# SiLUs of gate behind the last copy out of a bank, and V weights at multiples of 256 bytes, in a neighbourhood-attention and SwiGLU layer

## The chip, the cores and the metric

One core of a Trainium2 chip runs the whole program. The metric is the device time of one execution in microseconds (us). Three runs of the kernel before took 1791.04, 1791.50 and 1793.87 us, so its median is 1791.5.

## The reference

One encoder layer is applied to two groups of tokens with the same parameters, 1024 tokens (`x_prompt`) and 512 (`x_sample`), with 1024 features, 16 heads of 64 and 2816 columns in the feed-forward part. All is float32.

```python
def swiglu(x, w_gate, w_up, w_down):
    return (jax.nn.silu(x @ w_gate) * (x @ w_up)) @ w_down

def run(x):
    h = rms_norm(x, norm_mix)
    x = x + neighbourhood_attention(h, na_w_qkv, na_rpb, na_w_o)
    x = x + swiglu(rms_norm(x, norm_ffn), w_gate, w_up, w_down)
    return rms_norm(x, norm_final)
```

`neighbourhood_attention` projects `h` to q, k and v, and lets each token of a grid 64 wide attend to a window of at most 8 rows and 16 columns, with a bias that depends on the offset. With the depth of one layer that is set here, the other mixers of the reference don't run.

## The kernel before

Tokens are taken in tiles of 128. A float32 matrix is split in two parts, `hi` (rounded, made by a cast on ACT) and `lo` (the rest, a subtraction on DVE; `split`, L155 to L161), and a product is three matmuls for each block of 128 rows: hi hi, hi lo, lo hi (`PASS`, L180). The stages follow one another on TensorE (PE):

- **V projection** (L303 to L341, 10 to 159 us). The norm of twelve token tiles is made and transposed, and `v_tile` (L292) multiplies each by the 512 columns of one half of the V weights, first half `n = 0`, then half `n = 1`: 24 matmuls a tile, with the transposed tokens (`hTp`, `hTs`) as the stationary and the weights (`wv`) as the moving operand of 512 columns. The pool `vpool` (L261) holds in this order `fill` (480 numbers in each partition, the value of a masked bias, written out by DMA at L320), the norm's gains `gb`, two `x`, five `wv0`, five `wv1` and two `vs`. Its first byte is a multiple of 256 in each partition. Raw weights of half `n = 1` come through a pool of two buffers (`rpool`, L164).
- **Attention** (159 to 800 us): q and k projections (L351), scores (L413), transposes (L439), weighted sums (L450), and the output projection (L609).
- **Gate and up** (L934 to L949, 800 to 1460 us). Tokens are in two chunks of 768, the feature blocks in 11 pairs, so there are 22 calls of `unit`, here counted 0 to 21 in the order in which they run. A unit computes a 2 x 2 block product by seven products in place of eight (Strassen's method in Winograd's form), once for gate and once for up (`blocks`, L847). A product is 12 matmuls with a moving operand of 384 columns, and sums are kept in the PSUM banks `pa`, `pb` and `pd`:

| step of `blocks` | PE | out of the bank |
|---|---|---|
| 1 | product 0 into `pa` | ACT copies `pa` to `c11` (L858) |
| 2 | product 1 into `pb` | DVE adds `pb` to `c11` (L861) |
| 3 | product 5 onto `pa` | ACT copies `pa` to `c12` (L865) |
| 4 | product 4 into `pd` | ACT copies `pd` to `c22` (L869) |
| 5 | product 6 onto `pa` | DVE adds `pa` to `c22` (L872) |
| 6 | product 2 onto `pd` | DVE adds `pd` to `c12` (L875) |
| 7 | product 3 onto `pa` | stays there, read by the last SiLU |

 A product that goes on in a bank must wait until what stands there has been read: product 6 for the copy to `c12`, product 2 for the copy to `c22`, product 3 for the add to `c22`. After gate's seventh step `unit` writes the four SiLUs (L892) in the order c11, c12, `pa`, c22 of its list `gs`; after up's it multiplies (L896). GpSimd (POOL) then adds four operands of the next stage (L900 to L903) and issues seven stores (L905). Between the steps `ticks` runs a little of other work: in chunk 0 norms and transposes of chunk 1, in chunk 1 `down_sums` (L770), sums of down's weights on DVE (L784, L786) and POOL (L789, L791). The operands of a block's products are made in `w_ops` (L803): `wa` from one piece of the weights, `ws` from two sums `wt`.
- **Down** (L1063 to L1122, 1460 to 1789 us), 1386 matmuls, again seven products a block.

The order in which each engine takes its instructions is set before the run, by a scheduler that knows what depends on what and may move an instruction ahead of others on the same engine; a dependency of the kind `NoSync` between two instructions of one engine (as in `in_order`, L98, and `pinned`, L110) is no wait of its own, but keeps their order. On the chip an engine takes them one by one, and one that waits holds up those behind it.

Of the kernel before, what the change touches and what calls it, by code (L numbers as in the profile page):

```python
# [11 lines left out]
F32 = mybir.dt.float32  # L12
F32R = mybir.dt.float32r
AF = mybir.ActivationFunctionType
# [4 lines left out]
P = 128  # L19
# [36 lines left out]
def body(tc, xp, xs, g_mix, g_ffn, g_fin, w_qkv, rpb, w_o, w_g, w_u, w_d, yp, ys):  # L56
    nc = tc.nc
# [8 lines left out]
    with es:  # L66
# [43 lines left out]
        def pinned(work, *engines):  # L110

            traced = nc.cur_bb.bb.instructions
            mark = traced[-1]
            done = next(work, 0) == 0
            start = next(k for k in reversed(range(len(traced))) if traced[k] is mark) + 1
            for e in engines:
                own = [i for i in traced[start:] if i.engine == e.engine]
                if own:
                    last = next((i for i in reversed(traced[:start]) if i.engine == e.engine), None)
                    for a, b in zip([last] + own, own):  # L120
                        if a is not None:
                            tc.add_manual_dep(b, a.name, mybir.DependencyInfo(
                                mybir.DependencyClass.NoSync, mybir.DependencyReason.DATA), reason="pinned")
            return done

        def psum(tag, name):
            return ps.tile([P, 512], F32, tag=tag, name=name, bufs=4 if tag == "S" else 2)
# [131 lines left out]


        with tc.tile_pool(name="vpool", bufs=2) as vp:  # L261
            fill = vp.tile([P, 480], F32, tag="fill", name="fill", bufs=1)
            nc.gpsimd.memset(fill, FILL)
            gb = vp.tile([P, D], F32, tag="gb", name="gb", bufs=1)

# [363 lines left out]
        for hp in range(HP):  # L629
# [5 lines left out]
            n = len(jobs[hp])  # L635
# [201 lines left out]
        def product(bank, a, b, start, stop):  # L837
            for k in range(KB // 2):
                for i, (y, z) in enumerate(PASS):
                    nc.tensor.matmul(bank[:, :HT], a(y, k), b[:, z, k], start=start and k == 0 and i == 0,  # L840
                                     stop=k == KB // 2 - 1 and i == 2,
                                     skip_group_check=not start)

        def ctile():
            return fl.tile([P, HT], F32, tag="c", name="c", bufs=13)

        def blocks(w, p, hops, out):  # L847

            ops = w_ops(w, p)
            pa, pb, pd = psum("G", "pa"), psum("V", "pb"), psum("S", "pd")  # L850
            va, vb, vd = pa[:, :HT], pb[:, :HT], pd[:, :HT]

            def go(i, bank, start, stop):
                product(bank, ops[i], hops[i], start, stop)

            go(0, pa, True, False)
            c11 = ctile()
            nc.scalar.copy(c11, va)  # L858
            yield
            go(1, pb, True, True)  # L860
            nc.vector.tensor_tensor(c11, c11, vb, ALU.add)  # L861
            yield
            go(5, pa, False, False)
            c12 = ctile()
            nc.scalar.copy(c12, va)  # L865
            yield
            go(4, pd, True, False)
            c22 = ctile()
            nc.scalar.copy(c22, vd)  # L869
            yield  # L870
            go(6, pa, False, False)
            nc.vector.tensor_tensor(c22, c22, va, ALU.add)  # L872
            yield
            go(2, pd, False, True)
            nc.vector.tensor_tensor(c12, c12, vd, ALU.add)  # L875
            yield
            go(3, pa, False, True)
            out.extend((c11, c12, va, c22))
            yield

        def unit(c, p, hops, tick):
            gs, us = [], []
# [3 lines left out]
            for x in order:  # L886
                next((g, u)[x])
                done[x] += 1
                if not x and done[0] == 7:
                    for n in (0, 1, 3, 2):  # L890
                        o = ctile() if n == 2 else gs[n]
                        nc.scalar.activation(o, gs[n], AF.Silu)  # L892
                        gs[n] = o
                tick()
            for n in (0, 1, 3, 2):
# [156 lines left out]
        c11, c12, c22 = {}, {}, {}  # L1052
# [10 lines left out]
        for q in range(84):  # L1063
            m, tt, h = q // 12, q % 12 // 2, q % 2
            n = SEQ[m]
# [76 lines left out]
```

## Time and profile before

| | |
|---|---|
| median of three runs | 1791.5 us |
| the profiled execution, its own time | 1791.51 us |
| its span, first to last instruction | 1789.4 us |
| mean granted TensorE clock | 0.994 |
| gate and up, first to last matmul | 799.65 to 1460.24 us |
| busy share of ACT / DVE / POOL | 49% / 68% / 25% |

```profile
DVE  4401787778887666677777877877888866546553
ACT  4411667677776455445454434543434335433433
PEclk9999999999999999999999999999999999999999
```

These are three rows of the page's slices: each digit is the busy share of one 40th of the span (44.7 us) in tenths, and the last row is TensorE's granted clock. Neither DVE nor ACT is full in gate and up (digits 18 to 33), so what counts there is whether one of their instructions is late, not how many there are.

In the rows of the timeline that follow below, the columns are start and length in us, the engine, the line of the kernel, the operation, and out<-in by the names of the program; brackets at a row's end give the idle time before it and what ended it.

### The profile page before, as it was taken

The page shows a single profiled execution, that of the slowest core. Times are in us where ns is not written, and L with a number is a line of the kernel's source. Part 1 is how long each engine was busy: PE and PEld are TensorE (multiplying, and loading weights), DVE is VectorE, ACT ScalarE, POOL GpSimd, SP SyncE. Part 2 cuts the span into 40 slices and gives each one's busy share as a digit, 9 for nine tenths or more (in the row PEclk, how much of TensorE's full clock was granted, in tenths as well). Part 3 has the DMA queues.
Part 4 walks back from the last instruction along what each step waited for, and adds up shares of the span by engine and source line. Part 5 has one row for each costly group of instructions (what it writes and reads, how often), then busy time and mean ns, then how long its engine had stood idle before and what let it go on. Part 6 is the DMA issues. An engine that isn't in the chain of part 4 may idle for free.

```text
span 1789.4 us, 25908 instructions
## 1 busy us (share of the span) xinstructions
PE 1735.7 (97%) x9178; PEld 1522.1 (85%) x9178; DVE 1211.5 (68%) x2267; ACT 870.4 (49%) x1742; POOL 439.5 (25%) x509
## 2 busy tenths in 40 slices
PE   7999999999999999999999999999999989999998
PEld 6878777777776878879999999999999978888886
DVE  4401787778887666677777877877888866546553
ACT  4411667677776455445454434543434335433433
POOL 1111000000121000112443424344545462005300
PEclk9999999999999999999999999999999999999999
DMA  7755333333464444554545633554666469555643
GB/s 243 220 173 175 110 104 106 105 113 106 127 195 154 146 133 136 181 161 150 159 151 164 217 112 124 182 171 158 206 228 217 171 218 340 184 166 166 211 119 110
DMA packets 229858, 295.60 MB, mean 165 GB/s; under 512 B 27648, under 2 KB 173824, under 8 KB 229728
## 3 DMA queue, kind: packets, MB, share of 16 engines
q1 hardware_dynamic: 205744, 215.94, 39.3%
q0 software_dynamic: 21248, 69.62, 10.6%
q10 hardware_dynamic: 2736, 8.39, 1.4%
q8 instruction: 72, 1.18, 0.3%
q14 instruction: 58, 0.48, 0.1%
HBM read 218.45 MB, written 87.97 MB: 171 GB/s over the span
## 4 chain that ended last, share of the span: by engine, by line
PE 72%; DVE 10%; DMA 8%; ACT 4%; issue 3%; SPq 1%; POOL 1%; DVEq 0%; ACTq 0%; POOLq 0%
PE pd L1078 17%; PE pa L840 16%; PE pg L351 8%; PE pd L840 8%; PE pgv L297 6%; PE pgo L609 5%; PE pb L840 4%; DMA vr<-v_d 4%; PE pss L413 3%; PE po L450 2%; PE ptt L439 2%; DMA wr<-na_w_qkv 1%; SPq L397 1%; ACT s L424 1%; DVE pT L443 1%
## 5 line engine op out<-in xcount | busy, mean ns | idle before, releaser
L1078 PE MATMUL pd<-wd,go 128*128 128x512 f32 x1386 | 317.9, 392 | 3.8 <-DVE wd L158 3.1
L1078 PEld LDWEIGHTS pd<-wd,go 128*128 128x128 f32 x1386 | 261.9, 189 | 59.8 <-DVE wd L158 4.3
L840 PE MATMUL pa<-h,ws 128*128 128x384 f32 x1056 | 200.0, 337 | 8.0 <-ACT c L865 7.2
L351 PE MATMUL pg<-hTp,whl 128*128 128x512 f32 x768 | 200.7, 405 | 0.0
L840 PE MATMUL pd<-h,ws 128*128 128x384 f32 x1056 | 197.4, 334 | 0.0
L840 PEld LDWEIGHTS pa<-h,ws 128*128 128x128 f32 x1056 | 183.1, 188 | 12.8 <-ACT c L865 10.8
L840 PEld LDWEIGHTS pd<-h,ws 128*128 128x128 f32 x1056 | 184.3, 188 | 0.0
L158 DVE TENSOR_TENSOR ws<-wt,ws 128x1024 fp32r<-128x1024 f32 x88 | 118.5, 1348 | 83.8 <-ACT ws L157 83.7
L351 PEld LDWEIGHTS pg<-hTp,whl 128*128 128x128 f32 x768 | 138.9, 190 | 33.7 <-issue 7.7
L840 PE MATMUL pa<-h,wa 128*128 128x384 f32 x792 | 146.0, 335 | 1.8 <-DVE c L872 1.8
L609 PE MATMUL pgo<-wo,oh 128*128 128x512 f32 x576 | 139.1, 392 | 1.3 <-DVE oh L158 1.3
L840 PEld LDWEIGHTS pa<-h,wa 128*128 128x128 f32 x792 | 137.6, 188 | 2.8 <-DVE c L872 2.7
L424 ACT ACTIVATE s<-s,mx 128x384 f32<-128x384 f32 (+1 forms) x192 | 109.0, 570 | 55.3 <-DVE mx L421 55.3
L157 ACT CAST go<-gr 128x768 fp32r<-128x768 f32 x84 | 65.6, 783 | 137.5 <-PE pd L1078 97.9
L158 DVE TENSOR_TENSOR go<-gr,go 128x768 fp32r<-128x768 f32 x84 | 81.6, 972 | 70.1 <-ACT go L157 68.7
L609 PEld LDWEIGHTS pgo<-wo,oh 128*128 128x128 f32 x576 | 107.4, 188 | 24.6 <-DVE oh L158 1.7
L905 POOL DMA_DIRECT2D gop_d<-c x66 | 50.6, 767 | 304.1 <-DVE c L896 296.9
L158 DVE TENSOR_TENSOR wa<-wr,wa 128x512 fp32r<-128x512 f32 x132 | 112.5, 864 | 18.9 <-ACT wa L157 18.0
L157 ACT CAST ws<-wt 128x1024 fp32r<-128x1024 f32 x88 | 92.5, 1053 | 64.6 <-issue 52.4
L157 ACT CAST wa<-wr 128x512 fp32r<-128x512 f32 x132 | 81.9, 621 | 71.5 <-PE pb L840 43.6
L351 PE MATMUL pg<-hTs,whl 128*128 128x512 f32 x384 | 107.3, 416 | 2.1 <-DVE q L362 2.1
L840 PE MATMUL pb<-h,wa 128*128 128x384 f32 x528 | 98.6, 334 | 0.0
(158 smaller groups left out, 2953.3 us busy)
## 6 DMA issues: line engine op xcount, KB each, us to landing
wr<-ffn_w_gate SPq DMA_DIRECT2D x44, 512.0 KB
wr<-ffn_w_up SPq DMA_DIRECT2D x44, 512.0 KB
wr<-na_w_qkv SPq DMA_DIRECT2D x38, 512.0 KB
gop_d<-gs POOLq DMA_DIRECT2D x88, 192.0 KB, 4.7
gr<-gop_d SPq DMA_DIRECT2D x42, 384.0 KB
gr<-gop_d SPq DMA_DIRECT2D x42, 320.0 KB
gop_d<-c POOLq DMA_DIRECT2D x66, 192.0 KB, 2.7
vr<-v_d SPq DMA_DIRECT2D x192, 64.0 KB
```

Of the source, the lines that this page charges most:

```text
L157: nc.scalar.copy(hi, raw)
L158: nc.vector.tensor_tensor(lo, raw, f32(hi), ALU.subtract)
L297: nc.tensor.matmul(pg, hh[a][:, k, c:c + P], wv[k // 2][b][:, k % 2], start=(k == 0 and i == 0), stop=(k == KB - 1 and i == 2))
L351: nc.tensor.matmul(pg, w[:, a, k, :], h[b][:, k, c:c + 512], start=(k == 0 and i == 0), stop=(k == KB - 1 and i == 2))
L413: nc.tensor.matmul(pt[:, :n], q[h * HD:(h + 1) * HD, a, j].rearrange("p r i -> p (r i)"), kv[:, krow:krow + nrow, BS[j]:BS[j] + 32], start ...
L424: nc.scalar.activation(s[:, :n], s[:, :n], AF.Exp, bias=mx, scale=-1.0, accum_out=sm)
L439: nc.tensor.transpose(pt[:, c * P:(c + 1) * P], s[:, c * P:(c + 1) * P], ident)
L450: nc.tensor.matmul(pos[h][:, g * 256:(g + 1) * 256], vs[c][:, j, h * P:(h + 1) * P], pT[h][:, c].rearrange("p z q -> p (z q)"), start=(c = ...
L609: nc.tensor.matmul(pg, ohs[k // 4][:, a, k % 4], wo[:, b, k, n * 512:(n + 1) * 512], start=(k == 0 and i == 0), stop=(k == KB - 1 and i == 2))
L840: nc.tensor.matmul(bank[:, :HT], a(y, k), b[:, z, k], start=start and k == 0 and i == 0, stop=k == KB // 2 - 1 and i == 2, skip_group_chec ...
L905: nc.gpsimd.dma_start(out=gop_d[i, 3 * c:3 * c + 3, :, p].rearrange("j q t -> q j t"), in_=a.rearrange("q (j t) -> q j t", j=3))
L1078: nc.tensor.matmul(pd, go[:, y, i - a], wds[m, i][:, z], start=(i == 0 and k == 0), stop=(i == NP - 1 and k == 2))
```

## The change

Two edits. In `unit`, each of the four SiLUs of gate is given an order on ACT behind `copied[0]`, which is the last instruction that `blocks` wrote at its fourth step, the copy of `pd` to `c22`; at that place gate's blocks have run and up's have not, so it is gate's own copy. And `fill` is given 512 numbers a partition, of which 480 are used as before, so that every later tile of `vpool` lies 128 bytes further on.

```diff
+        def after(ins, *others):
+
+            for o in others:
+                tc.add_manual_dep(ins.ins, o.ins.name, mybir.DependencyInfo(
+                    mybir.DependencyClass.NoSync, mybir.DependencyReason.DATA), reason="after")
...
-            fill = vp.tile([P, 480], F32, tag="fill", name="fill", bufs=1)
+            fill = vp.tile([P, 512], F32, tag="fill", name="fill", bufs=1)[:, :480]
...
+        copied = [None]
+
...
             c22 = ctile()
-            nc.scalar.copy(c22, vd)
+            copied[0] = nc.scalar.copy(c22, vd)
...
-                        nc.scalar.activation(o, gs[n], AF.Silu)
+                        after(nc.scalar.activation(o, gs[n], AF.Silu), copied[0])
```

In the built programs the `wv` tiles start at byte 115,072 of a partition before and 115,200 after, each next one 4,096 further on: 128 past a multiple of 256 before, on one after. The tiles `hTp`, `whl`, `wo`, `oh`, `wd` and the operands `h`, which the other projections read, start on multiples of 256 in both. PE's, POOL's and SP's instructions stand in the same order as before; ACT's differ in the 22 gates, DVE's in a few of them.

On ACT, a gate without other work beside it (such as that of unit 20), before, from its copy of `pa` to `c11` on. `wa` and `ws` are the cast operands, `c<-pa` and `c<-pd` the copies, ACTIVATE the SiLUs:

```order
L858 COPY c<-pa 128x384
L157 CAST wa<-wr 128x512 x2
L892 ACTIVATE c<-c 128x384
L865 COPY c<-pa 128x384
L869 COPY c<-pd 128x384
L157 CAST ws<-wt 128x1024
L892 ACTIVATE c<-c 128x384
L157 CAST ws<-wt 128x1024
```

The same gate with the change (line numbers are up to 8 higher there):

```order
L866 COPY c<-pa 128x384
L163 CAST wa<-wr 128x512 x2
L873 COPY c<-pa 128x384
L877 COPY c<-pd 128x384
L900 ACTIVATE c<-c 128x384
L163 CAST ws<-wt 128x1024
L900 ACTIVATE c<-c 128x384
L163 CAST ws<-wt 128x1024
```

The first SiLU has moved past both copies; it now stands between the copy to `c22` and the first cast of `ws`. This is so in all gates but those of units 1, 3 and 5.

On ACT, the gate of unit 3, which has two squares of a norm beside it (L696, with the tile numbers 9914 and 9915), before, from behind the first copy:

```order
L892 ACTIVATE c<-c 128x384
L157 CAST wa<-wr 128x512
L865 COPY c<-pa 128x384
L157 CAST wa<-wr 128x512
L869 COPY c<-pd 128x384
L696 ACTIVATE t_9914,ms<-t_9916 128x1024
L696 ACTIVATE t_9915,ms<-t_9917 128x1024
L157 CAST ws<-wt 128x1024
L892 ACTIVATE c<-c 128x384
L157 CAST ws<-wt 128x1024
```

With the change:

```order
L163 CAST wa<-wr 128x512 x2
L873 COPY c<-pa 128x384
L877 COPY c<-pd 128x384
L702 ACTIVATE t_9914,ms<-t_9916 128x1024
L702 ACTIVATE t_9915,ms<-t_9917 128x1024
L900 ACTIVATE c<-c 128x384 x2
L163 CAST ws<-wt 128x1024 x2
```

Here two SiLUs stand behind the squares and ahead of both casts of `ws`.

On DVE, the same gate of unit 3, before, from the add of `pb` on (L861; `me` belongs to the norm):

```order
L861 TENSOR_TENSOR c<-c,pb 128x384
L158 TENSOR_TENSOR wa<-wr,wa 128x512 x2
L698 TENSOR_SCALAR me<-ms 128x1
L872 TENSOR_TENSOR c<-c,pa 128x384
L158 TENSOR_TENSOR ws<-wt,ws 128x1024
L875 TENSOR_TENSOR c<-c,pd 128x384
L698 TENSOR_SCALAR me<-ms 128x1
L158 TENSOR_TENSOR ws<-wt,ws 128x1024
```

With the change:

```order
L869 TENSOR_TENSOR c<-c,pb 128x384
L164 TENSOR_TENSOR wa<-wr,wa 128x512 x2
L704 TENSOR_SCALAR me<-ms 128x1
L880 TENSOR_TENSOR c<-c,pa 128x384
L883 TENSOR_TENSOR c<-c,pd 128x384
L704 TENSOR_SCALAR me<-ms 128x1
L164 TENSOR_TENSOR ws<-wt,ws 128x1024 x2
```

Both adds out of PSUM now stand ahead of both subtractions for `ws`.

## The prediction

> **What bounds the kernel now.** I read the page first, for the engine that is full and for the chain of work that ended last.
>
> ```profile
> PE 1735.7 (97%) x9178; PEld 1522.1 (85%) x9178; DVE 1211.5 (68%) x2267; ACT 870.4 (49%) x1742; POOL 439.5 (25%) x509
> ...
> PE pd L1078 17%; PE pa L840 16%; PE pg L351 8%; PE pd L840 8%; PE pgv L297 6%; PE pgo L609 5%; PE pb L840 4%; DMA vr<-v_d 4%; PE pss L413 3%; PE po L450 2%; PE ptt L439 2%; DMA wr<-na_w_qkv 1%; SPq L397 1%; ACT s L424 1%; DVE pT L443 1%
> ```
>
> PE is the bound, and both edits touch lines that stand high in the chain: V projection (L297) and gate and up (L840). There a shorter matmul, or a stop of PE that goes, counts in full unless something else is late right behind it. Second, the groups, for what stops PE in gate and up:
>
> ```profile
> L840 PE MATMUL pa<-h,ws 128*128 128x384 f32 x1056 | 200.0, 337 | 8.0 <-ACT c L865 7.2 <-ACT c L858 0.8
> ...
> L840 PE MATMUL pa<-h,wa 128*128 128x384 f32 x792 | 146.0, 335 | 1.8 <-DVE c L872 1.8
> ```
>
> The 7.2 us are product 6 waiting for the copy to c12 (L865), the 1.8 us product 3 waiting for the add to c22 (L872). Third, the timeline of one such stop, the gate of unit 21:
>
> ```profile
> 1435.82 2.25 PE L840 MATMUL pd<-h,ws 128*128 128x384 f32 x12
> ...
> 1437.98 0.54 DVE L861 TENSOR_TENSOR c<-c,pb 128x384 f32<-128x384 f32 x1
> ...
> 1438.55 0.52 ACT L892 ACTIVATE c<-c 128x384 f32<-128x384 f32 x1 [4.00 <-DVE c L861]
> 1438.98 0.46 ACT L865 COPY c<-pa 128x384 f32<-128x384 f32 x1
> ...
> 1439.50 2.36 PE L840 MATMUL pa<-h,ws 128*128 128x384 f32 x12 [1.43 <-ACT c L865]
> 1439.71 1.06 ACT L157 CAST ws<-wt 128x1024 fp32r<-128x1024 f32 x1
> 1440.68 1.31 POOL L791 TENSOR_TENSOR t<-t 128x512 f32<-128x512 f32 x1
> 1440.81 2.27 DVE L158 TENSOR_TENSOR ws<-wt,ws 128x1024 fp32r<-128x1024 f32 x1 [1.69 <-ACT ws L157]
> ...
> 1443.00 0.54 DVE L872 TENSOR_TENSOR c<-c,pa 128x384 f32<-128x384 f32 x1
> ...
> 1443.78 2.24 PE L840 MATMUL pa<-h,wa 128*128 128x384 f32 x12
> ```
>
> What the copy reads, product 5, was ready when product 4 began at 1435.82. But ACT stood for 4.00 us at the SiLU, which waits for DVE's late add (L861), and the copy stood behind it. A product takes 2.08 us where nothing stops PE (the chain's row at 813.40 in part 2: 24 matmuls in 4.16), so product 6 was **due** at 1435.82 + 2.08 = 1437.90 and came 1.60 late: the bracket's 1.43 and 0.17 to start again. It also runs 0.12 longer after the stop (2.36, and 2.24 for product 3 at 1443.78).
>
> **Part 1: the SiLU behind the copy to c22.** Nothing is added or removed; the SiLU moves past both copies and now stands ahead of the cast of `ws`, so the new question is what that cast delays: DVE's subtraction for `ws`, and behind it on DVE the add L872, for which product 3 waits. A plain gate without a stop, unit 8, gives the steps:
>
> ```profile
> 1049.55 0.52 ACT L892 ACTIVATE c<-c 128x384 f32<-128x384 f32 x1 [2.39 <-DVE c L861]
> ...
> 1049.98 0.46 ACT L865 COPY c<-pa 128x384 f32<-128x384 f32 x1
> ...
> 1050.51 2.35 PE L840 MATMUL pa<-h,ws 128*128 128x384 f32 x12
> 1050.75 0.48 ACT L869 COPY c<-pd 128x384 f32<-128x384 f32 x1 [0.30 <-issue]
> 1051.13 1.05 ACT L157 CAST ws<-wt 128x1024 fp32r<-128x1024 f32 x1
> 1052.21 1.23 DVE L158 TENSOR_TENSOR ws<-wt,ws 128x1024 fp32r<-128x1024 f32 x1 [2.09 <-ACT ws L157]
> ...
> 1053.35 0.55 DVE L872 TENSOR_TENSOR c<-c,pa 128x384 f32<-128x384 f32 x1
> ```
>
> Call T the start of product 6. Copy to c22 at T + 0.24, next instruction 0.38 later, SiLU 0.43 (start to start), so the cast at T + 1.05 in place of T + 0.62; the subtraction 1.08 later, L872 1.14 after that, T + 3.27; product 3 may start 0.60 after L872 does (unit 18 below), T + 3.87. Due is T + 4.16, so 0.29 us of slack is left and PE hides the move. What such a gate gains is the 0.11 by which its product 6 runs long (2.35): seven gates (8, 9, 10, 12, 13, 14, 19), **0.7 us**. The rest of the stopped gates:
>
> ```profile
> 899.24 2.37 PE L840 MATMUL pa<-h,ws 128*128 128x384 f32 x12 [0.84 <-ACT c L865]
> ...
> 960.61 2.35 PE L840 MATMUL pa<-h,ws 128*128 128x384 f32 x12 [1.05 <-ACT c L865]
> ...
> 1021.25 2.38 PE L840 MATMUL pa<-h,ws 128*128 128x384 f32 x12 [0.33 <-ACT c L865]
> ...
> 1024.27 0.54 DVE L872 TENSOR_TENSOR c<-c,pa 128x384 f32<-128x384 f32 x1
> ...
> 1143.83 0.54 DVE L872 TENSOR_TENSOR c<-c,pa 128x384 f32<-128x384 f32 x1
> ...
> 1257.69 2.36 PE L840 MATMUL pa<-h,ws 128*128 128x384 f32 x12 [0.33 <-ACT c L865]
> ...
> 1258.88 1.30 POOL L789 TENSOR_TENSOR t<-t,t 128x512 f32<-128x512 f32 x1
> 1259.00 2.27 DVE L158 TENSOR_TENSOR ws<-wt,ws 128x1024 fp32r<-128x1024 f32 x1 [1.08 <-ACT ws L157]
> ...
> 1261.19 0.54 DVE L872 TENSOR_TENSOR c<-c,pa 128x384 f32<-128x384 f32 x1
> ...
> 1288.53 2.36 PE L840 MATMUL pa<-h,ws 128*128 128x384 f32 x12 [1.44 <-ACT c L865]
> ...
> 1353.23 0.54 DVE L872 TENSOR_TENSOR c<-c,pa 128x384 f32<-128x384 f32 x1
> ...
> 1353.83 2.37 PE L840 MATMUL pa<-h,wa 128*128 128x384 f32 x12 [1.32 <-DVE c L872]
> ```
>
> - Unit 21. T = 1437.90; SiLU at 1438.55 as before (its add), cast at 1438.98, subtraction at 1440.06, ahead of POOL's add at 1440.68, so it takes the 1.23 of unit 8 and not 2.27. L872 at 1441.20, PE free to go at 1441.80, due 1442.06: no stop, and product 3 comes 1443.78 - 1442.06 = **1.72** earlier. Unit 16 reads alike: **1.72**.
> - Units 3 and 5: 0.84 + 0.17 + 0.12 and 1.05 + 0.17 + 0.12, **2.5**. On DVE L872 now stands ahead of the subtraction for `ws`, which is needed only by up's third product.
> - Unit 7: T = 1020.75, due 1024.91; L872 stays at 1024.27 (no idle time before it, so DVE's own queue sets it) and lets PE go at 1024.87: **0.6**.
> - Unit 15, and 20 like it: T = 1257.20, cast at 1258.25, subtraction at 1259.33 instead of 1259.00. POOL's add holds it up in both (2.27 for 1.23) and ends at 1260.18, so L872 stays at 1261.19; PE goes at 1261.79, not 1261.97: **0.2** each, though 0.49 of stop and more seem to go.
> - Units 11 and 18: L872 at 1143.83 and 1353.23 comes out of a DVE that has no idle time before it, and product 3 waits for it already; a stop only moves from product 6 to product 3: **0**. Unit 17 likewise (and may lose 0.1). Units 0, 1, 2, 4, 6 don't wait here.
>
> Sum: 0.7 + 3.44 + 2.5 + 0.6 + 0.4 = **7.6 us**. Bounds: 10.5 if L872 is never late (nine brackets, 7.2, nine times 0.17 and 0.12, and the plain gates' 0.7), and 4.6 if units 16 and 21 too meet POOL's add and keep 0.2 each. I stay at 7.6, since the subtraction there starts 0.6 before POOL.
>
> The Trainium skill's page "SBUF — State Buffer" (SBUF: two separate sides) says that DVE and GpSimd share a port as an exclusive lock, and the loser waits for the whole instruction. The 2.27 against 1.23 agree; by a port that is shared out instead, units 15 and 20 would gain nothing and the sum would be 7.2.
>
> **Part 2: V's weights on multiples of 256 bytes.** Same instructions; only addresses move. The chain in order of time:
>
> ```profile
> 77.84 4.23 DMA wr<-na_w_qkv
> 84.44 7.75 DMA wr<-na_w_qkv
> 94.64 64.46 PE pgv L297 x275
> 159.10 21.80 PE pg L351 x96
> ...
> 778.03 21.78 PE pgo L609 x96
> ...
> 813.40 4.16 PE pa L840 x24
> ```
>
> With a moving operand of 512 columns PE takes 21.80 / 96 = 227 ns a matmul in q and k projection, 21.78 / 96 = 227 in the output projection, but 64.46 / 275 = 234 in V projection, the only one of the three whose moving tiles start off the 256 bytes. The chain stays on PE through those 64 us. So 7.4 ns x 275 = **2.0 us** in the second half. In the first half the chain runs from PE through two loads of weights (77.84, 84.44) into the second half: what PE gains before about 75 us moves them forward, what it gains later it waits out at 94. From 38 to 75 six tiles of 24 gain some 0.14 each (not every matmul, as each tile is broken by transposes): **0.8 us**. Earlier PE waits for norms. Sum 2.8; bounds 0, if the addresses aren't the cause, and 576 x 7.4 ns = 4.3. Attention starts on loads and biases issued in this stage, which move with it; the loads into the moved tiles I take at nothing (no row has one at both addresses).
>
> **Sum.** The profiled execution took 1791.51 us (span 1789.4), the median is 1791.5, so no correction: 1791.5 - 7.6 - 2.8 = **1781.1**.
>
> **The rivals.**
> - *A, addresses change nothing*: the 7 ns belong to something else in V projection, such as its stationary operand. For it: no row varies the address alone. Against: the stationary tiles (`hTp`) start on 256 in both programs, and all the moving tiles that run at 227 ns do. 1791.5 - 7.6 = 1783.9. The Trainium skill, "SBUF — State Buffer" (Specifications), gives SBUF lines of 16 bytes and a penalty for crossing into a new one; 128 bytes is a whole number of these, so by that rule a run of 2,048 bytes costs the same at both addresses, which is this rival. Its section on operand start alignment says that its runs timed nothing; the 227 against 234 here speak the other way.
> - *B, the stop is handed on*: in units 16 and 21 the subtraction for `ws` starts 0.6 us later than I replay, behind POOL's add; gain there 0.2 each, 4.6 in all, 1791.5 - 4.6 - 2.8 = 1784.1. For it: the cast has only 0.6 us in hand, less than one SiLU and a copy. Against: its inputs are there, and POOL's add comes behind five stores of its own queue.
> - *C, slower*: the SiLU ahead of the cast pushes DVE's subtraction into a POOL instruction in nearly every gate. Then L872 comes at T + 3.27 + 1.04, product 3 is 0.75 late, 22 x 0.75 = 16.5 us, against stops that now cost 7.2 + 1.8 and a dozen restarts of at most 0.29, some 12.5 in all: 4 us lost. With V's 2.8 about 1792.7, without it 1795.5. It decides from about 20 gates on. Against: POOL's adds lie there in units 15 to 18, 20 and 21 only.
> - *D, nothing*: PE's stops were L861's lateness and remain, since other casts hold the copies, and A holds too: 1791.5. Against: in unit 21 ACT sat idle for the 4.00 us ahead of the SiLU, so no cast ahead of it was late.
>
> **How the numbers follow.** Forecast 0.60 (1779 to 1783), A 0.13, B 0.17, C 0.04, D 0.06. 0.2% is 3.6 us, about what a measurement of this kernel can tell from no change. Faster 0.60 + 0.13 + 0.17 = 0.90, same 0.06, slower 0.04. The three runs lie 2.8 us apart, and one stretch at a lower granted clock costs 1.5:
>
> ```profile
> 331.86 4.52 PE pg L351 x12
> 343.17 2.99 PE pg L351 x12
> ```
>
> So the range takes the upper bounds of both parts (1791.5 - 10.5 - 4.3 = 1776.7) at the low end, and A and B and one or two such stretches at the high end: 1776.7 to 1786.5.
>
> **What would show it.** Second half of V projection 62.4 us long and 227 ns a matmul; waits of PE for L865 near 0; waits for L872 up from 1.8 to about 4.3 (units 11, 15, 17, 18, 20); `ws` cast about 0.4 later behind product 6; units 3, 5, 7, 16, 21 near 29.1 us. Wrong, if L872 waits reach 9, if V stays at 234 ns, or if the gain is lost at the start of down (L1078), where loads set the pace.

## The result, and the profile after

The changed kernel took 1783.47 us (median of four runs, 1780.15 to 1785.13) beside 1792.03 for the kernel before (four runs, 1791.04 to 1793.87): a ratio of 0.9948, 95% interval 0.993 to 0.9966, that is 8.6 us less. The ratio is estimated over the runs of both kernels, so it need not be the quotient of two medians. One run of the kernel before, in the rows of e10 and e11 below, took 6000.42 us and is left out of the median there. The changed kernel's profiled execution took 1784.12 us, with a span of 1782.1 (before 1789.4).

Lines have moved by 6 to 8: gate and up's matmul is L846 (before L840), V projection's L303 (L297), the copy to c11 L866 (L858), the add to c11 L869 (L861), the copies to c12 and c22 L873 and L877 (L865, L869), the add to c22 L880 (L872), the SiLU L900 (L892), cast and subtraction of `split` L163 and L164 (L157, L158). From the page of the changed kernel, engines, the chain by line and the two groups of gate and up in which PE waits (busy time, mean ns of one, idle time ahead of it and what ended it):

```profile
PE 1729.5 (97%) x9178; PEld 1521.2 (85%) x9178; DVE 1207.1 (68%) x2267; ACT 870.7 (49%) x1742; POOL 439.1 (25%) x509
...
PE pa L846 18%; PE pd L1086 17%; PE pd L846 8%; PE pg L357 7%; PE pgv L303 6%; DMA vr<-v_d 5%; PE pb L846 4%; PE pgo L615 4%; PE pss L419 3%; DMA wr<-na_w_qkv 2%; SPq L403 2%; PE po L456 2%; PE ptt L445 1%; ACT s L430 1%; DVE pT L449 1%
...
L846 PE MATMUL pa<-h,ws 128*128 128x384 f32 x1056 | 198.0, 335 | 2.3 <-ACT c L866 2.3
...
L846 PE MATMUL pa<-h,wa 128*128 128x384 f32 x792 | 147.2, 337 | 3.6 <-DVE c L880 3.6
```

PE is still the bound and the same lines carry the chain. The 7.2 us for the copy to c12 are gone from the first group; what stands there now, 2.3 for the copy to c11, is another wait (unit 11, below). The wait for the add to c22 has doubled, 1.8 to 3.6. The gate of unit 21, in time:

```profile
1432.92 2.24 PE L846 MATMUL pa<-h,ws 128*128 128x384 f32 x12
1433.00 0.54 DVE L869 TENSOR_TENSOR c<-c,pb 128x384 f32<-128x384 f32 x1
1433.16 0.48 ACT L877 COPY c<-pd 128x384 f32<-128x384 f32 x1 [1.65 <-PE pd L846]
...
1433.58 0.53 ACT L900 ACTIVATE c<-c 128x384 f32<-128x384 f32 x1
1434.01 1.03 ACT L163 CAST ws<-wt 128x1024 fp32r<-128x1024 f32 x1
...
1435.00 0.68 PE L846 MATMUL pd<-h,ws 128*128 128x384 f32 x3
1435.07 1.31 DVE L164 TENSOR_TENSOR ws<-wt,ws 128x1024 fp32r<-128x1024 f32 x1 [0.93 <-ACT ws L163]
```

DVE's add to c11 comes as late as before, 0.08 us after product 6 begins, but nothing that PE needs waits for it: the copy to c22 stands ahead of the SiLU, product 6 begins without a bracket, and the subtraction runs 1.31 us, not 2.27. In V projection the chain's row of the second half is shorter:

```profile
94.09 62.73 PE pgv L303 x275
```

62.73 / 275 = 228.1 ns a matmul, where it was 234. By stages the profiled execution lies against that of before like this (last or first matmul of each): end of V projection -2.27 us, start of gate and up -1.47, its end -6.70, end of the span -7.3. So V gave 2.3, attention took 0.8 back, gate and up gave 5.2, down 0.6. In attention PE stood 2.1 us longer than before (24.95 for 22.86), with one stretch at half clock fewer (two for three).

Lengths of single units, first matmul to first matmul of the next, against the profile of before (the last column is the first experiment):

| units | forecast | changed kernel | SiLUs alone |
|---|---|---|---|
| 8, 9, 10, 12, 13, 14, 19, each | -0.11 | -0.10 to -0.11 | -0.10 to -0.11 |
| 16 and 21, each | -1.72 | -1.72 | -1.72 |
| 3 and 5 together | -2.5 | -2.47 | -2.47 |
| 7 | -0.6 | -0.57 | -0.55 |
| 15, 20 | -0.2 each | -0.05, -0.06 | -0.04, -0.05 |
| 11 | 0 | +0.94 | -0.04 |
| 17 | 0 | 0.00 | +0.02 |
| 18 | 0 | +1.55 | +0.01 |
| 0 | 0 | -0.41 | -0.21 |
| sum | -7.6 | -5.2 | -7.5 |

The two units that are longer are the ones where the forecast had nothing: 11 and 18. Unit 18 in the changed kernel, product 3 after its wait, and then four stretches of 3.41 us around it (columns: stretch, its length, busy us of PE, PEld, DVE, ACT and POOL with their instructions, granted clock, share of the DMA engines, GB/s):

```profile
1344.24 1.62 POOL L797 TENSOR_TENSOR t<-t 128x512 f32<-128x512 f32 x1
1344.65 2.30 DVE L164 TENSOR_TENSOR ws<-wt,ws 128x1024 fp32r<-128x1024 f32 x1
1346.87 0.54 DVE L880 TENSOR_TENSOR c<-c,pa 128x384 f32<-128x384 f32 x1
...
1347.47 2.98 PE L846 MATMUL pa<-h,wa 128*128 128x384 f32 x11 [1.95 <-DVE c L880]
```

```profile
1341.75:1345.16 3.41, 3.41 (x21) 3.41 (x20) 3.41 (x3) 1.52 (x3) 3.31 (x4) 1.00 0.97 332
1345.16:1348.58 3.42, 1.47 (x9) 1.15 (x8) 3.42 (x5) 1.13 (x2) 0.71 (x1) 1.00 0.58 194
1348.58:1351.99 3.41, 3.41 (x13) 3.41 (x12) 3.04 (x5) 1.75 (x4) 0.00 (x0) 0.50 0.95 322
1351.99:1355.40 3.41, 3.41 (x22) 3.41 (x21) 1.27 (x2) 1.00 (x2) 0.00 (x0) 1.00 0.29 115
```

In the third stretch the granted clock is 0.50 and PE ends 13 matmuls instead of 21 or 22: that is the 1.55 us. In the kernel before PE stood about as long in this unit, but in two pieces that began 4.8 us apart, 0.33 at product 6 and the 1.32 at product 3 that the prediction shows; the first piece:

```profile
1348.05 2.38 PE L840 MATMUL pa<-h,ws 128*128 128x384 f32 x12 [0.33 <-ACT c L865]
```

No slow stretch followed there. Whether the slow stretch belongs to the change is a question for the experiments.

### The profile page after: what moved, and what is told of

The parts are those of the page before. It is cut to its first block, busy times and chain, and to the rows that moved or that the text cites. A ratio compares the mean times of both kernels' runs of the same rounds, so it can differ in the third digit from the quotient of the medians.

```text
span 1782.1 us, 25923 instructions
## 1 busy us (share of the span) xinstructions
PE 1729.5 (97%) x9178; PEld 1521.2 (85%) x9178; DVE 1207.1 (68%) x2267; ACT 870.7 (49%) x1742; POOL 439.1 (25%) x509
## 4 chain that ended last, share of the span: by engine, by line
PE 71%; DVE 9%; DMA 9%; ACT 5%; issue 4%; SPq 2%; POOL 1%; DVEq 0%; ACTq 0%; POOLq 0%
PE pa L846 18%; PE pd L1086 17%; PE pd L846 8%; PE pg L357 7%; PE pgv L303 6%; DMA vr<-v_d 5%; PE pb L846 4%; PE pgo L615 4%; PE pss L419 3%; DMA wr<-na_w_qkv 2%; SPq L403 2%; PE po L456 2%; PE ptt L445 1%; ACT s L430 1%; DVE pT L449 1%
## 5 line engine op out<-in xcount | busy, mean ns | idle before, releaser
L846 PE MATMUL pa<-h,ws 128*128 128x384 f32 x1056 | 198.0, 335 | 2.3 <-ACT c L866 2.3
L846 PE MATMUL pd<-h,ws 128*128 128x384 f32 x1056 | 197.4, 334 | 0.0
L846 PEld LDWEIGHTS pa<-h,ws 128*128 128x128 f32 x1056 | 183.9, 188 | 2.9 <-ACT c L866 2.9
L846 PEld LDWEIGHTS pd<-h,ws 128*128 128x128 f32 x1056 | 184.3, 188 | 0.0
L164 DVE TENSOR_TENSOR ws<-wt,ws 128x1024 fp32r<-128x1024 f32 x88 | 114.5, 1305 | 78.6 <-ACT ws L163 78.5
L846 PE MATMUL pa<-h,wa 128*128 128x384 f32 x792 | 147.2, 337 | 3.6 <-DVE c L880 3.6
L846 PEld LDWEIGHTS pa<-h,wa 128*128 128x128 f32 x792 | 138.2, 189 | 5.4 <-DVE c L880 5.2
L163 ACT CAST go<-gr 128x768 fp32r<-128x768 f32 x84 | 65.6, 783 | 138.9 <-PE pd L1086 101.6
L164 DVE TENSOR_TENSOR go<-gr,go 128x768 fp32r<-128x768 f32 x84 | 81.8, 975 | 69.3 <-ACT go L163 67.9
L163 ACT CAST ws<-wt 128x1024 fp32r<-128x1024 f32 x88 | 91.8, 1048 | 59.3 <-issue 52.7
L164 DVE TENSOR_TENSOR wa<-wr,wa 128x512 fp32r<-128x512 f32 x132 | 110.4, 852 | 15.1 <-ACT wa L163 14.6
L163 ACT CAST wa<-wr 128x512 fp32r<-128x512 f32 x132 | 81.8, 621 | 74.8 <-PE pb L846 41.3
L846 PE MATMUL pb<-h,wa 128*128 128x384 f32 x528 | 98.6, 334 | 0.0
```

The lines of the kernel that those rows point to most:

```text
L163: nc.scalar.copy(hi, raw)
L164: nc.vector.tensor_tensor(lo, raw, f32(hi), ALU.subtract)
```

## The experiments

The times of one row were taken on the same chip; where a kernel ran once, no interval is given.

| run | us | kernel before beside it | ratio, 95% interval |
|---|---|---|---|
| e1_silu_only | 1781.43 (7 runs) | 1787.07 | 0.9964, 0.9949 to 0.9978 |
| e2_align_only | 1783.00 (12) | 1787.07 | 0.9977, 0.9966 to 0.9988 |
| e3_both | 1781.09 (7) | 1787.07 | 0.9964, 0.995 to 0.9978 |
| e4_add_first | 1772.77 (6) | 1787.07 | 0.9923, 0.9907 to 0.994 |
| e5_silu_behind_cast | 1778.90 (10) | 1788.36 | 0.9945, 0.9929 to 0.9961 |
| e6_copy_twice | 1781.68 (1) | 1788.36 | |
| e8_fill496 | 1786.84 (1) | 1788.36 | |
| e9_fill488 | 1783.34 (1) | 1788.36 | |
| e10_add_first_576 | 1774.79 (6) | 1786.36 | 0.9933, 0.9908 to 0.9958 |
| e11_stops | 1783.21 (1) | 1786.36 | |
| e12_stops | 1785.50 (1) | 1791.19 | |
| e13_stops | 1792.13 (1) | 1785.27 | |

### The two parts, apart and together

The SiLUs alone:

```diff
-            fill = vp.tile([P, 512], F32, tag="fill", name="fill", bufs=1)[:, :480]
+            fill = vp.tile([P, 480], F32, tag="fill", name="fill", bufs=1)
```

> The new kernel with the fill tile back at 480 columns, so that V's weights lie 128 bytes past a multiple of 256 as before; only the SiLUs' place is changed. My theory (both parts work, and add): gate and up is 5 to 7 us shorter than in the kernel before, the wait of PE for the copy to c12 is gone, the second half of V's projection stays at 234 ns a matmul (64.5 us), and the time is 5 to 7.6 us below the kernel before, about 1785.5. Rival (the SiLUs bring it all, the address nothing): the time equals that of the kernel with both parts, about 1783.5. Rival (the SiLUs bring nothing): 1791 to 1792.

The addresses alone:

```diff
-                        after(nc.scalar.activation(o, gs[n], AF.Silu), copied[0])
+                        nc.scalar.activation(o, gs[n], AF.Silu)
```

> The new kernel with the SiLUs issued as before; only V's weights lie at multiples of 256 bytes. My theory: the second half of V's projection takes about 62.7 us instead of 64.5 (228 instead of 234 ns a matmul), the first half about 0.5 us less, PE still waits about 7 us for the copy to c12 in gate and up, and the time is 1.7 to 2.8 us below the kernel before, about 1789.7. Rival (the address does nothing, the shift in V is a whim of that execution): V at 234 ns and 1791.5 to 1792. Rival (the address brings the whole gain): about 1783.5.

The changed kernel once more:

> The changed kernel as it is, again, on the same chip as the parts. My theory: 8 to 9 us below the kernel before, and its gain is the sum of the two parts' gains to within 1 us. Where the clock's half-speed stretches fall differs from run to run, so the profile of this run should show the unit that was 1.55 us longer in the first profile (unit 18, matmuls at half the clock) and unit 11 (0.94 us, ACT held by a transfer) in another place or not at all; if the unit 11 stop comes back the same, it belongs to the new order and not to the run.

Of e1, the matmuls of one group of gate and up, which hold its first and its last (first and last start in us), V's row of the chain, and the two groups of gate and up in which PE waits:

```profile
L846 PE MATMUL pa<-h,wa x792: 333/334/445, 798.0 to 1451.1; 128*128 128x384 f32 x198
...
85.80 73.87 PE pgv L303 x317
...
L846 PE MATMUL pa<-h,ws 128*128 128x384 f32 x1056 | 198.0, 335 | 0.7 <-ACT c L866 0.6
...
L846 PE MATMUL pa<-h,wa 128*128 128x384 f32 x792 | 146.3, 336 | 4.5 <-DVE c L880 4.5
```

The same of e2, with the first of the two groups:

```profile
L846 PE MATMUL pa<-h,wa x792: 333/334/444, 789.6 to 1449.9; 128*128 128x384 f32 x198
...
94.71 61.27 PE pgv L303 x269
...
L846 PE MATMUL pa<-h,ws 128*128 128x384 f32 x1056 | 199.8, 337 | 8.0 <-ACT c L873 7.4
```

Gate and up runs 653.1 us in e1 and 660.3 in e2, against 660.6 before (799.65 to 1460.24). V runs at 73.87 / 317 = 233.0 ns in e1 and at 61.27 / 269 = 227.8 in e2, and its last matmul starts at 159.28 in e1, 155.59 in e2, 155.61 in e3. The wait for the copy to c12 (L873) is whole in e2 and absent in e1. So each part works alone and does what the forecast said: the order 7.5 us in gate and up, the address about 3 at the end of V (before 158.70). That the addresses change nothing (rival A) is out, and so is that the stops remain (D).

By total times the sum is not seen, and my expectation of e3 (8 to 9 us) is missed: 6.4 us and 4.1 us for the parts (ratios times 1787), 6.4 for both. The intervals are some 2.5 us wide to either side, so they allow 9 for both as well, which the first chip gave. The profile of e3 shows where some of it may lie: its gate and up ends 6.1 us shorter, not 7.5, and this time it is unit 11 that is 1.51 longer, with a stretch at half clock at 1137.0; unit 18 is as before (+0.02). In the first profile it was unit 18 at half clock, in e1 neither. Attention alone, from V's last matmul to the first of gate and up, takes 634.0 (e2) to 641.8 us (the first profile of the changed kernel) over the 14 profiles, though no engine's order of instructions differs between them there. Single executions thus differ by nearly as much as the whole change is worth, and the stages tell more than the totals. The slow stretch in gate and up is not in every execution of the new order; what it hangs on is the last experiment's question.

### Which address

Fill tiles of other sizes put V's weights elsewhere: 496 columns at 192 bytes past a multiple of 256, 488 at 160.

```diff
-            fill = vp.tile([P, 512], F32, tag="fill", name="fill", bufs=1)[:, :480]
+            fill = vp.tile([P, 496], F32, tag="fill", name="fill", bufs=1)[:, :480]
```

> Both parts' code, but the fill tile takes 496 columns, which puts V's weights at 192 bytes past a multiple of 256 (before: 128 past; changed kernel: 0 past). My theory (a row of 2048 bytes that does not start on a multiple of 256 touches one block of 256 bytes more, and each matmul pays for it): the second half of V's projection takes about 64.5 us as in the kernel before, 234 ns a matmul. Rival (the step is at 64 bytes): 62.7 us, 228 ns, as in the changed kernel. Gate and up is another execution of the new order: 7.5 us shorter than before, but for half-speed stretches.

> As the one with 496 columns, but 488, which puts V's weights 160 bytes past a multiple of 256, and so 32 past a multiple of 64. My theory: 234 ns a matmul in the second half of V's projection, 64.5 us. Rival (the step is at 32 bytes or less): 228 ns, 62.7 us. Rival (each 64 bytes has its price): more than 234 ns here, or a rate between the two.

The chain's row of V in e8:

```profile
84.72 74.14 PE pgv L303 x317
```

and in e9:

```profile
85.08 74.38 PE pgv L303 x317
```

74.14 / 317 = 233.9 ns and 74.38 / 317 = 234.6: slow at 192 and at 160, as at 128. A multiple of 128, of 64 or of 32 is not enough. e10 below, with 576 columns, lies on a multiple of 256 that is not one of 512, and its row is fast again (61.27 / 269 = 227.8):

```profile
94.80 61.27 PE pgv L303 x269
```

So on these five addresses the step is at 256 bytes, and the price of missing it is 5 to 7 ns a matmul of 512 columns. All 14 profiles agree: from one start to the next, the median matmul of the second half takes 227 ns in the ten with a multiple of 256 and 232 to 234 in the four without. That a row of 2,048 bytes then touches a ninth block of 256 fits this, but nothing here shows what the reading hardware does. Nor is the address all that counts: the q and k projections, whose moving tiles stay on multiples of 256, run their first 96 matmuls at 227 ns, but later ones, mixed with the rest of attention, at a median of 233, in the kernel before and in the changed one alike. What costs them that is not shown.

### What holds product 3

In the changed kernel PE waits at product 3 in units 15, 17, 18 and 20, and the forecast gave units 15 and 20 more than they brought. Two ways to change what stands ahead of the add to c22: take the SiLU from in front of ACT's cast (e5), or take DVE's subtraction from in front of the add (e4).

```diff
-                if not x and done[0] == 7:
+                if x and done[1] == 1:
...
-                        after(nc.scalar.activation(o, gs[n], AF.Silu), copied[0])
+                        after(nc.scalar.activation(o, gs[n], AF.Silu), casts[-2])
```

> Both parts, but the SiLUs of gate are issued one step later still: behind ACT's cast of up's first operand instead of ahead of it. My theory (the cast, and so DVE's subtraction and the addition to c22 behind it, is late by the one SiLU that stands ahead of it): the cast is back at 0.62 us after product 6 begins, the addition starts about 0.42 us earlier, the waits of PE at product 3 in units 15, 17 and 20 (0.43 to 0.55) shrink to 0.1 or less and that in unit 18 from 2.1 to about 1.7; nothing else waits for the SiLUs, so gate and up is 9 to 9.6 us shorter than in the kernel before, where the changed kernel's was 7.5 shorter outside half-speed stretches. Rival (the addition is held by POOL's hold on DVE's subtraction alone): the waits at product 3 stay as they are, 7.5. Rival (the last SiLU, now behind up's copy to c11, lets gate's bank go later): new waits of PE in gate's or up's first product, over 3 us in all.

```diff
+                if w is w_u:
+                    after(lo, added[0])
...
-            nc.vector.tensor_tensor(c22, c22, va, ALU.add)
+            added[0] = nc.vector.tensor_tensor(c22, c22, va, ALU.add)
```

(`lo` is the subtraction that `split` issues for `ws`.)

> Both parts, and in gate's product chains DVE does the addition to c22 before the subtraction that makes the rounded remainder of up's first operand (in the changed kernel the subtraction may come ahead of it). My theory: the waits of PE at product 3 for the addition (0.43 in units 15 and 20, 0.54 in 17, 0.9 in 11, up to 2.1 in 18) go, the new place of the subtraction is about 1.2 us later but still 0.9 us or more ahead of up's first product that needs it, so 2 to 4 us less than the kernel with both parts: about 1780.5. Rival: up's first operand is now late in most gates and PE stops there instead, some 0.3 us in each of 22 units: 6 us slower than both, about 1790. Rival: nothing changes (within 1 us of both), because ACT's copy, not DVE's subtraction, holds the addition.

Unit 15 in e5, where product 6 begins at 1248.18, and under it in the changed kernel, where it begins at 1252.61:

```profile
1248.80 1.05 ACT L163 CAST ws<-wt 128x1024 fp32r<-128x1024 f32 x1
...
1249.86 1.30 POOL L796 TENSOR_TENSOR t<-t,t 128x512 f32<-128x512 f32 x1
1249.88 2.37 DVE L164 TENSOR_TENSOR ws<-wt,ws 128x1024 fp32r<-128x1024 f32 x1 [0.98 <-ACT ws L163]
...
1252.17 0.54 DVE L881 TENSOR_TENSOR c<-c,pa 128x384 f32<-128x384 f32 x1
```

```profile
1253.65 1.04 ACT L163 CAST ws<-wt 128x1024 fp32r<-128x1024 f32 x1
1254.28 1.30 POOL L795 TENSOR_TENSOR t<-t,t 128x512 f32<-128x512 f32 x1
...
1254.72 1.95 DVE L164 TENSOR_TENSOR ws<-wt,ws 128x1024 fp32r<-128x1024 f32 x1 [1.40 <-ACT ws L163]
...
1256.60 0.54 DVE L880 TENSOR_TENSOR c<-c,pa 128x384 f32<-128x384 f32 x1
```

The cast comes 0.42 us earlier in e5 (0.62 behind product 6, not 1.04), the subtraction too, but it takes 2.37 instead of 1.95 and the add stays at 3.99 behind product 6 in both. The subtraction ends 1.09 us after POOL's add does in both. So my expectation of e5 falls, and its first rival holds: in this gate POOL sets the time, not ACT. Gate and up was 8.1 us shorter than before, 0.5 of the difference to e1 in unit 11. In e4 the add no longer stands behind that subtraction; unit 18 there, product 6 at 1332.18:

```profile
1333.93 1.81 DVE L790 TENSOR_TENSOR t<-t 128x512 f32<-128x512 f32 x1
...
1335.66 0.54 DVE L883 TENSOR_TENSOR c<-c,pa 128x384 f32<-128x384 f32 x1
1336.13 1.85 DVE L164 TENSOR_TENSOR ws<-wt,ws 128x1024 fp32r<-128x1024 f32 x1
...
1336.35 1.39 PE L848 MATMUL pa<-h,wa 128*128 128x384 f32 x7
```

Product 3 starts on time, 4.17 behind product 6, where it started 6.28 behind it in the changed kernel. Units 15, 17, 18 and 20 are 0.6, 0.7, 2.2 and 0.6 shorter than before the change, the others keep what they had, PE waits nowhere for the later `ws`, and gate and up runs 649.0 us. Unit 11 keeps a stop of 1.8 us for the add to c22, which I had expected to go as well.

```profile
L848 PE MATMUL pa<-h,wa x792: 333/334/445, 791.2 to 1440.2; 128*128 128x384 f32 x198
```

That is 11.6 less than before and 4.1 less than with the SiLUs alone, and by its median this version beats both kernels. The median lies 8.3 us under that of e3, though, and gate and up explains 5.5 of it in the two profiles (654.5 in e3); the 4.5 us by which e4's profile is ahead when gate and up begins come from attention, which the edit does not touch. The same order with the other address:

> The kernel with the addition ahead of the subtraction, now with a fill tile of 576 columns instead of 512: V's weights lie on a multiple of 256 bytes that is not one of 512. My theory (256 bytes is the step): V's second half at 227 to 228 ns a matmul (62.4 to 62.7 us), gate and up 11.6 us shorter than in the kernel before, time equal to the earlier run of this order within 2 us (about 1773). Rival (the step is 512 bytes): V at 234 ns, 64.5 us, and about 3 us more.

It took 1774.79 us; gate and up was 9.9 us shorter, not 11.6, as unit 11 had a stretch at half clock again (+1.58).

### The slack at product 3

```diff
             copied[0] = nc.scalar.copy(c22, vd)
+            if w is w_g:
+                copied[0] = nc.scalar.copy(c22, vd)
```

> Both parts, and in gate's chains ACT writes the copy to c22 twice (one more copy of 0.48 us between product 4's end and up's first cast). This prices the slack that the forecast gave product 3 in the plain units, 0.29 us. My theory: in the seven plain units (8, 9, 10, 12, 13, 14, 19) PE now waits 0.1 to 0.25 us at product 3, in units 15, 17, 18 and 20 some 0.3 to 0.5 more than before the doubling, in units 16 and 21 about 0.3; in all 3 to 4.5 us more in gate and up. Rival (the slack is larger, or ACT's queue has a hole that takes the copy up): under 1 us more. Rival (the copy moves a conflict with POOL onto the plain units): over 6 us more.

Unit 8, product 2 and what it waits for:

```profile
1043.98 1.05 ACT L163 CAST ws<-wt 128x1024 fp32r<-128x1024 f32 x1
1044.93 0.48 ACT L879 COPY c<-pd 128x384 f32<-128x384 f32 x1
...
1045.46 2.37 PE L846 MATMUL pd<-h,ws 128*128 128x384 f32 x12
```

The scheduler took the cast ahead of the second copy, so it is product 2 that now waits for `pd` to be read, and the plain units' 0.16 us are the price of that. It says nothing on product 3. (That units 15 and 20 lose nothing by it does fit: there the next wait is set by POOL.) The slack is read from the changed kernel instead, unit 8, where product 6 begins at 1045.59:

```profile
1048.85 0.55 DVE L880 TENSOR_TENSOR c<-c,pa 128x384 f32<-128x384 f32 x1
...
1049.75 4.32 PE L846 MATMUL pa<-h,wa 128*128 128x384 f32 x24
```

The add lies at 3.26 and product 3 at 4.16; with the 0.60 from one to the other (1346.87 to 1347.47 in unit 18) 0.30 us are left, forecast 0.29.

### Half clock behind a stop

Over all profiles the stretches at half clock begin on a grid of 3.413 us, at another offset in each execution. I made stops of PE to see whether they follow stops, with more copies to c22 in single gates.

```diff
+            if w is w_g:
+                for _ in range({8: 7, 10: 7, 13: 7, 19: 7, 9: 4, 12: 4, 14: 4}.get(gates[0], 0)):
+                    copied[0] = nc.scalar.copy(c22, vd)
+                gates[0] += 1
```

> The changed kernel, with made stops of PE: in the gates of units 8, 10, 13 and 19 ACT writes the copy to c22 seven times more, in those of units 9, 12 and 14 four times more, 0.38 us each, less the 0.22 us of slack that the doubled copy left: stops of about 2.4 us at product 3 in the first four units, about 1.3 us in the other three. My theory (the clock is set anew every 3.413 us, and a stretch in which PE stood for over some 1.8 us is followed by one at half speed; where the stretches begin against the program differs from run to run): two or three of the four long stops, chance 0.66 each, are followed by a stretch at half speed within 3.4 us, which makes the unit some 1.5 us longer beyond its stop; none of the three short ones is. Rival (half-speed stretches come whatever PE does): none in these seven units, as in ten profiles so far. Rival (only a stop of a whole stretch, 3.4 us, brings it): none as well.

The second time up's casts of `ws` were held behind the copies (`after(cast, copied[0])`); the third time this stayed, and the numbers were 11 and 9 in place of 7 and 4.

> The made stops again, now with up's first cast held behind the added copies on ACT (in the run before, ACT took that cast first, and the stops came out at 0.57 and 0.29 us): seven copies more in gate of units 8, 10, 13 and 19, four more in 9, 12 and 14. By 0.16 us for one added copy and 0.38 for each further, PE stops about 2.4 us at product 3 in the first four and 1.3 in the others. In the twelve profiles so far a stretch of 3.413 us in which PE stood 1.83 us or more was followed by one at half speed 25 times out of 25 in all, and in gate and up no stretch in which it stood under 1.5 us was. My theory: of the four long stops those that lie with 1.83 us or more in one stretch (two or three, chance 0.66 each) are followed by a stretch at half speed and lengthen their unit by some 1.5 us beyond the stop; none of the short ones is. Rival (half-speed stretches come at these places of the program, whatever the stop): none in these seven units. Rival (only a stop of a whole stretch, 3.4 us): none.

> The made stops a third time, longer: with seven added copies units 8, 10, 13 and 19 were only 0.5 us longer than in the changed kernel (seven copies took 3.56 us, 0.51 each, and most of it lay beside product 6). Now eleven more copies in those four units and nine more in 9, 12 and 14. Each copy beyond the seventh should lengthen the stop by its 0.51 us, and a cast that now comes between them by 0.5: stops of 2.2 to 2.8 us in the first four units and 1.1 to 1.7 in the other three. My theory: as before, two or three of the four long stops put 1.83 us or more into one stretch of 3.413 us and are followed by one at half speed; of the short ones none that puts under 1.5 us into a stretch is. Rival (the half-speed stretches belong to places of the program): none in these seven units.

The stops did not get the lengths I wanted. In e11 the units were 0.57 and 0.29 us longer than in the changed kernel, in e12 some 0.5 and 0.34 (0.76 in unit 19), in e13 0.94 and 0.76. The scheduler had changed PE's order too: in these gates it took up's product 0, and in many of them product 1 as well, ahead of product 2, so PE worked on while ACT copied; in e11 and e13 ACT also took casts between the copies. None of these short stops is followed by half clock. But in unit 10 of e13 PE stood 2.0 us from one matmul to the next, and there it is, in a unit that had none in thirteen profiles; product 2 in time, and the stretches around it:

```profile
1106.79 2.24 PE L849 MATMUL pb<-h,wa 128*128 128x384 f32 x12
1110.83 3.12 PE L849 MATMUL pd<-h,ws 128*128 128x384 f32 x12 [1.80 <-ACT c L883]
```

```profile
1108.80:1112.20 3.40, 1.60 (x10) 1.37 (x9) 2.78 (x5) 3.40 (x7) 0.00 (x0) 1.00 0.58 147
1112.20:1115.61 3.41, 3.41 (x12) 3.41 (x11) 2.82 (x4) 2.71 (x5) 0.00 (x0) 0.50 0.56 203
1115.61:1119.02 3.41, 3.41 (x19) 3.13 (x19) 2.65 (x5) 2.25 (x5) 0.00 (x0) 1.00 0.39 115
```

One stop made on purpose is little. The count over all 14 profiles, with PE's idle time in each stretch of the grid worked out from the matmuls, is more. Of the stretches (themselves at full clock) in which PE stood 1.83 us or more, 30 of 30 were followed by one at half clock; of those with 1.5 to 1.83 us, the made stop with its 1.80 among them, 11 of 27; with 1.0 to 1.5 none of 93; with 0.8 to 1.0 eight of some 85, all in attention; and below 0.8 none. The bounds of these classes were chosen after the fact. In gate and up there are nine such cases: unit 18 (four profiles), 11 (four) and 10 (the made one). At the start of down PE stands 1.83 to 2.91 us in one stretch in all 14 profiles, with the change and without, and half clock follows each time. Units 11 and 18 are the only ones of gate and up with a stop of about 2 us that nobody made, and whether most of it falls into one stretch depends on the grid.

This ties the slow stretches to the change. From one matmul to the next, PE's stops in unit 18 were 0.49 and 1.49 us in the kernel before and 0.49 and 1.52 in e2, 4.8 us apart; in all ten profiles with the SiLUs' new place and without e4's order on DVE they are one stop of 2.0 to 2.1 us, and in four of the ten half clock follows. In unit 11 it was 1.27 and 0.33 before; now it is mostly one, up to 2.1 (3.0 in e13), and half clock follows in four of twelve. In e4 and e10 unit 18 has no stop and no slow stretch. Per execution that is 0.4 and 0.33 times some 1.55 us, about 1.1 us that the new order pays on average (an estimate from these counts; the two profiles of the old order alone would be few to say that it never pays).

## Why the prediction came out

The forecast was 1781.1 us, likeliest range 1779 to 1783, whole range 1776.7 to 1786.5. The time was 1783.47, inside the whole range and 0.5 above the likeliest; the gain was 8.6 us where the sum gave 10.4.

- **What bounds**: right. The stops of PE that went in units 3, 5, 7, 16 and 21 showed in the length of these units, to 0.05 us.
- **Part 1, the replay**: right in its steps. In unit 8 cast, add and product 3 lie at 1.04, 3.26 and 4.16 behind product 6 (forecast 1.05, 3.27, 4.16). Units 3, 5, 7, 16, 21 and the seven plain ones gave 7.2 us of 7.2. The sum of 7.6 stands at 7.5 in e1. Rival B (units 16 and 21 lose to POOL) and C (the slower one, POOL in nearly every gate) did not come; as the forecast read it, POOL's adds lie in a few units only. One sign was misread: units 3 and 5 could not come out near 29.1 us, since 30.62 and 30.80 less the forecast's own terms give 29.5, which is what they took (29.48 and 29.47).
- **Units 15 and 20**: mis-sized, 0.05 each for 0.2. The add to c22 stays where it was, as forecast; but the product that waits still has to start again after its stop. The forecast counted that 0.12 us where a stop goes and not where one stays. So small a gain is near the nothing that the forecast gave for a port that is shared out; but by e5's rows the subtraction ends at the same moment even when it begins earlier, which speaks against sharing.
- **Units 11, 17, 18**: this is the step that failed. "A stop only moves from product 6 to product 3: 0" is right for the stops (-0.04, +0.02, +0.01 in e1), but in 18, and mostly in 11, a stop that moves joins the one already there, and one stop of 2 us can bring a stretch at half clock where two smaller ones did not: 1.55 us in unit 18 of the first profile. The +0.94 in unit 11 is something else: ACT's copy to c11 stood behind a cast of a reloaded operand, which waited for its load (`t<-hop_d`). The same wait came again in e11 (1.71 us), while six of the other profiles of the new order were 0.04 to 0.51 shorter there than before, so it differs from execution to execution.
- **Part 2**: right in kind and near in size. The second half gave 64.46 - 62.73 = 1.73 us for 2.0, 6.3 ns a matmul for 7.4; the whole stage 2.3 in the first profile and 3.1 in e2 and e3, for 2.8.
- **The sum**: the terms hold (7.5 and about 3), the total came 1.8 us short on the first chip. In the first profile the gap is +1.55 in unit 18 (half clock), +0.94 in unit 11 (a load) and +0.8 in attention, which the forecast took at nothing and whose cause is not shown; over the profiles attention's length varies by far more, so the 0.8 cannot be called a price of the change. The forecast put stretches at half clock in the range and not in the sum, as chance alone. The grid is chance; the stop that it must meet was made by the change.
- **Waits for the add to c22**: 3.6 and in e1 4.5, for about 4.3.

What stays open: why the medians of e1 and e3 do not differ, though V ends 3.7 us earlier in e3. By the start of gate and up 2.3 us of the lead are left, with four stretches at half clock in e3's attention and three in e1's. The mean granted clock of e3's seven runs was 0.9936 and of e1's 0.9953, and 0.0017 of 1,780 us is 3 us; but seven runs do not show that this is more than the luck of the grid, and no mechanism was found that ties it to the address.

## What to carry to other kernels

Replay the moved instruction engine by engine from one clean period of the trace, down to what stands behind it in the queue; here that gave single units to 0.15 us wherever no stretch at half clock and no wait for a load fell. When a wait is handed on and not removed, look next at the engine whose queue holds the last releaser: putting one DVE add ahead of a subtraction that PE did not need yet brought 4 us more than the SiLUs' 7.5 in gate and up. Judge a change of a few us by the stage that it touches: here attention, in which no order was changed, differed by up to 8 us between executions. Two stops of PE that merge can cost more than their sum: in this kernel one of about 2 us was followed by a stretch at half clock in a third or more of the executions, some 1.5 us on top.

## What the runs showed of the hardware

- In V projection a matmul of 512 columns of float32 is 5 to 7 ns slower (233.0 to 234.6 for 227.8 to 228.1 ns) when its moving operand starts 128, 160 or 192 bytes past a multiple of 256 in each partition, and fast on an odd multiple of 256 as on a multiple of 512.
- The granted clock changes between 1.00 and 0.50 on a grid of 3.413 us, and 1.83 us or more without matmuls in one stretch of it was followed by a slow one 30 times of 30. The Trainium skill, "TensorE: Matmul & The Clock Gate" (Part 1: The HAM clock gate), gives a free-running window of 4096 cycles, 3413 ns, and these traces agree; its rule that gaps over some 3.4 us bring the half clock is too mild for them, by the 1.95 us wait of unit 18.
- Where POOL's add began first, DVE's subtraction ended about 1.09 us after that add, whenever it began itself (1.95 us from 1254.72, 2.37 from 1249.88), which is the same moment behind product 6. Where the subtraction began first (1435.07, unit 21 of the changed kernel), it took 1.31 us, and POOL's add 1.83 (1.31 in the kernel before).
